# A two-layer NSA and MoBA trunk in fp32: values of two head pairs in one run, gate rows summed from parts, five raw buffers

## The chip, the cores and the metric

The kernel runs on one core of a Trainium2 chip. The metric is the device time of one execution in microseconds; the figure of before is the median of three runs. The profile shows five engines: TensorE (PE, with its weight loads as PEld), VectorE (DVE), ScalarE (ACT), GpSimd (POOL) and SyncE (SP), which issues most of the transfers.

## The reference

There are 256 tokens of width 1024 and two layers. Each layer takes shift, scale and gate from a condition vector (adaLN), normalizes x, runs a mixer and adds the gated result. Layer 0 is NSA attention (16 heads in 4 groups, with compressed keys and values, selected blocks and a window of 256); layer 1 is MoBA attention with one block of 256, so that its attention is causal attention over all 256 tokens.

```python
cond = jax.nn.silu(c)
for i in range(DEPTH):
    shift, scale, gate = jnp.split(cond @ ada_w[i] + ada_b[i], 3, axis=-1)
    h = rms_norm(x, norm_g[i]) * (1 + scale[:, None, :]) + shift[:, None, :]
    ...
        y = nsa_mixer(h, ...)   # layer 0
        y = moba_mixer(h, ...)  # layer 1
    x = x + gate[:, None, :] * y
# in a mixer
q, kc, vc, ks, vs, kw, vw, gl, z = split_cols(h @ w_in, [Q_W] + [KV_W] * 6 + [3 * N_HEADS, Q_W])
...
return gc[..., 0:1] * o_cmp + gc[..., 1:2] * o_slc + gc[..., 2:3] * o_win
...
return (o * jax.nn.silu(z)) @ w_out
```

## The kernel before

**Numbers.** Everything is fp32. A large product is made from two parts of each operand: a high part, rounded to the type fp32r (`hi`, a cast on ACT), and the rest (`lo`, a subtraction on DVE). Three products, high by high, high by low and low by high, are added up in PSUM. The weights come from HBM in pieces of 512 KB, 128 partitions by 1024 numbers, into the buffers `raw` (six of them) or, in the first quarter, `early`. `HT` holds the two parts of the transposed, normalized x; `qg` holds the parts of the gated attention output.

**Order.** No engine's program is written out by hand. The functions record operations, and `plan.issue` (L285 to L403) sets the order of each engine: it goes through simulated time, takes for each engine the operation that can start first, then by level (FIRST_OF_ALL, URGENT, CHAIN, FILL) and by key. The key is the number of the operation, shifted by the table `LATER_BY` (L42); the table `HOLD` (L55) gives some operations an earliest time. The operations of a `plan.group` stay together. Every recorded operation is emitted at one line, L406, so the profile tells them apart by tiles and not by lines. Buffers belong to rings (`plan.tag`, L480 on): 2 `acc` and 6 `ps` in PSUM, 6 `raw`, 4 `hi`, 4 `lo`, 5 `pT`. Which instruction stands where on an engine therefore depends on the tables, the ring sizes and the numbers of the operations.

**The start.** The lead loop (`for k in range(2)`, L1124) makes the scale and shift of the first 128 columns of layer 0, transposes the normalized x, writes its high part (ACT) and low part (DVE) to `HT`, and multiplies with the first pieces of `w_in`, which `parts_2d` (L1114) splits into two halves of 512 columns, each with a cast on ACT.

**Scale and shift.** `ada_ss` multiplies pieces of `ada_w` with `condz`, a column of the condition, in small products: the PE array is then used in tiles of 128 by 32 (the names `early,condz` and `raw,condz` in the profile).

**The gate row.** `ada_gate(l)` (L757) multiplies eight pieces of `ada_w` by the condition with eight scalar_tensor_tensor operations on DVE, which add up in the tile `gate` of 128 by 1024. Two fp32 products with a matrix of ones (`ps<-gate,ones`, 512 columns each) then sum it over the partitions, and ACT copies both halves back to `gate`. There is one gate row for each layer.

**Attention of layer 0.** There are 8 pairs of heads. `pair_a(i)` makes the scores (`KTA,qg`), the maxima and exponentials (DVE and ACT) and the transposed probabilities `pT`, and in the end calls `values` (`pT,VA`): eight fp32 products in array tiles of 128 by 64, which add to a PSUM tile that `Vbd` (`pcT,Vbd`, the compressed values) began; the tiles of two pairs are begun together. `gated` then multiplies with the z branch. The compression itself uses small products in tiles of 128 by 64 (`p,p` and `zT,p`).

**Layer 1** has the same frame without compression and selection: `pair_b` and `values_b`, then the products with `w_out`. After the last product the result is multiplied with the gate, added to x and written out.

Of the kernel before, what the change touches and what calls it, by code (L numbers as in the profile page):

```python
# [17 lines left out]
P = 128  # L18
# [38 lines left out]
    120: 16500, 167: 22100, 305: 52600, 312: 37600, 383: 32300, 385: 34800, 390: 48600, 395: 51100, 499: 79600,  # L57
    503: 79600, 951: 114700, 1239: 173400, 1371: 179400, 1543: 193600, 1558: 197000, 1625: 208400, 1715: 225000,
    1717: 227500, 1746: 205600, 2238: 273000,
# [13 lines left out]
class Plan:  # L73
# [159 lines left out]
    def _safe(tag, k):  # L233

        if k not in tag.known:
            held = tag.early | {k}
            end = max(tag.last[h] for h in held)
            tag.known[k] = all(
# [195 lines left out]
def kernel(  # L434
# [323 lines left out]
    def ada_gate(l):  # L758
# [10 lines left out]
        for s in range(2):  # L769
            t = tile_of("ps", 512)  # L770
            with plan.at(FILL):
                T.matmul(t, ones, gate[:, s * 512:(s + 1) * 512], start=True, stop=True)
                A.copy(gate[:, s * 512:(s + 1) * 512], t)
# [794 lines left out]
```

## Time and profile before

| | before |
|---|---|
| median of 3 runs | 308.71 us (308.33 to 309.14) |
| the profiled execution | 307.97 us |
| its span, from the first to the last instruction | 306.3 us |
| mean granted TensorE clock | 0.998 |
| PE busy | 297.5 us, 2097 records |
| PE weight loads busy | 242.2 us |
| DVE busy | 248.7 us, 736 instructions |
| ACT busy | 203.0 us, 484 instructions |
| transferred | 65.80 MB, mean 215 GB/s |

The profiled execution took 1.67 us more than its span: that lies ahead of the first and behind the last instruction. PE records overlap, since a product is drawn with its full latency: what a product costs in a stream is the distance from its start to the next start, not the length of its record. An fp32 product appears as two records in the timeline and as one row in the order of instructions.

### The profile page before, as it was taken

Reading aid. Unit: us, or ns where it says so; the run is one execution under the profiler, and the core shown is the slowest. Engines: PE = TensorE matmul, PEld = TensorE weight load, DVE = VectorE, ACT = ScalarE, POOL = GpSimd, SP = SyncE. Lnnn points to the kernel's source line nnn. Section 1 sums busy time; section 2 is a strip of 40 time slices with the busy share of each in tenths; the row PEclk is TensorE's granted clock in tenths of the full one; section 3 lists DMA queues with packets and bytes.
Section 4 is the critical chain, followed back from the end, with each engine's and each line's share of the span. In section 5 each row is a group of like instructions: output and inputs, shape, how many; then the busy total and the mean of one; then the engine's idle time right before and its main releaser. Section 6 shows DMA issues by size and latency. Waiting matters only on the chain.

```text
span 306.3 us, 6115 instructions
## 1 busy us (share of the span) xinstructions
PE 297.5 (97%) x2097; PEld 242.2 (79%) x2097; DVE 248.7 (81%) x736; ACT 203.0 (66%) x484; POOL 29.4 (10%) x100
## 2 busy tenths in 40 slices
PE   4999999999999999999999999999999999999995
PEld 4666777868878696878897788787788999878784
DVE  3674474678799988799999897797599999999664
ACT  4735244674937795679877985766566589999510
POOL 8128980000000000000000000000000000000000
PEclk9999999999999999999999999999999999999999
DMA  8999999699974294968558269036477780441002
GB/s 250 321 355 368 367 355 342 229 271 323 347 284 149 63 372 140 346 207 328 162 185 274 70 205 329 17 76 224 131 258 235 235 285 4 149 131 67 2 34 103
DMA packets 41099, 65.80 MB, mean 215 GB/s; under 512 B 4220, under 2 KB 20970, under 8 KB 41068
## 3 DMA queue, kind: packets, MB, share of 16 engines
q1 hardware_dynamic: 40708, 65.36, 65.0%
q8 instruction: 16, 0.26, 0.3%
q14 instruction: 15, 0.12, 0.1%
q10 hardware_dynamic: 168, 0.06, 0.1%
q0 software_dynamic: 192, 0.00, 0.0%
HBM read 64.36 MB, written 1.05 MB: 214 GB/s over the span
## 4 chain that ended last, share of the span: by engine, by line
PE 82%; DVE 6%; ACT 5%; DMA 4%; issue 2%; ACTq 0%; SPq 0%; DVEq 0%
PE ps L406 46%; PE acc L406 36%; DVE p L406 3%; ACT p L406 2%; DMA y<-in_ada_b_dram 2%; DMA early<-in_nsa_w_in_dram 1%; DMA raw<-in_nsa_w_out_dram 1%; DVE lo L406 1%; ACT pT L406 1%; ACT n_out L406 1%; DVE tiny L406 0%; ACT hi L406 0%; ACT HT L406 0%; ACT qg L406 0%; ACTq L406 0%
## 5 line engine op out<-in xcount | busy, mean ns | idle before, releaser
L406 ACT CAST hi<-raw 128x1024 fp32r<-128x1024 f32 (+1 forms) x48 | 49.2, 1027 | 17.1 <-PE acc L406 14.8
L406 DVE TENSOR_TENSOR lo<-raw,hi 128x1024 fp32r<-128x1024 f32 (+1 forms) x48 | 56.7, 1188 | 3.1 <-ACT hi L406 2.8
L406 ACT ACTIVATE p<-p,tiny 128x128 f32<-128x128 f32 (+1 forms) x96 | 43.2, 459 | 10.7 <-DVE tiny L406 10.6
L406 PE MATMUL acc<-hi,HT 128*128 128x512 f32 (+1 forms) x160 | 49.6, 383 | 0.0
L406 PE MATMUL acc<-HT,hi 128*128 128x256 f32 x192 | 39.1, 288 | 0.0
L406 PEld LDWEIGHTS acc<-hi,HT 128*128 128x128 f32 x160 | 28.8, 188 | 6.7 <-issue 1.2
L406 DVE CUSTOM_DVE_ANT_0 p<-ps,causal 128x128 f32<-128x128 f32 (+1 forms) x96 | 31.3, 356 | 1.5 <-PE ps L406 1.5
L406 PEld LDWEIGHTS acc<-HT,hi 128*128 128x128 f32 x192 | 30.5, 189 | 0.9 <-issue 0.7
L406 PE MATMUL acc<-lo,HT 128*128 128x512 f32 (+1 forms) x80 | 30.4, 384 | 0.4 <-DVE lo L406 0.4
L406 PE MATMUL ps<-hi,HT 128*128 128x512 f32 (+1 forms) x96 | 29.0, 367 | 0.0
L406 PE MATMUL ps<-KTA,qg 128*128 128x256 f32 (+2 forms) x192 | 27.3, 282 | 0.0
L406 PE MATMUL acc<-HT,lo 128*128 128x256 f32 x96 | 27.3, 286 | 0.0
L406 PEld LDWEIGHTS ps<-KTA,qg 128*128 128x128 f32 x192 | 24.2, 189 | 3.3 <-issue 1.2
L406 PE MATMUL ps<-hi,qg 128*128 128x256 f32 (+1 forms) x96 | 24.4, 324 | 0.0
L406 PE MATMUL acc<-hi,qg 128*128 128x512 f32 x64 | 23.3, 415 | 0.0
L406 ACT COPY pT<-ps 128x384 f32<-128x384 f32 x48 | 21.1, 492 | 2.3 <-PE ps L406 2.3
L406 DVE TENSOR_TENSOR lo<-early,hi 128x1024 fp32r<-128x1024 f32 (+2 forms) x17 | 17.4, 1041 | 5.4 <-ACT hi L406 5.0
L406 ACT CAST hi<-early 128x1024 fp32r<-128x1024 f32 (+2 forms) x17 | 14.8, 897 | 10.3 <-DMA early<-in_nsa_w_in_dram 8.5
L406 PE MATMUL ps<-identF,p 128*128 128x128 f32 x144 | 21.0, 275 | 0.2
L406 PEld LDWEIGHTS ps<-hi,HT 128*128 128x128 f32 x96 | 17.2, 188 | 4.6 <-issue 1.9
L406 DVE SCALAR_TENSOR_TENSOR gate<-raw,condz,gate 128x1024 f32<-128x1024 f32 x16 | 20.5, 1283 | 0.0
L406 PEld LDWEIGHTS ps<-identF,p 128*128 128x128 f32 x144 | 16.2, 140 | 3.8 <-DVE p L406 0.9
(218 smaller groups left out, 618.8 us busy)
## 6 DMA issues: line engine op xcount, KB each, us to landing
raw<-in_ada_w_dram SPq DMA_DIRECT2D x32, 512.0 KB, 5.7
raw<-in_moba_w_in_dram SPq DMA_DIRECT2D x20, 512.0 KB, 4.7
early<-in_ada_w_dram SPq DMA_DIRECT2D x12, 512.0 KB, 9.6
raw<-in_nsa_w_in_dram SPq DMA_DIRECT2D x12, 512.0 KB, 6.6
early<-in_nsa_w_in_dram SPq DMA_DIRECT2D x9, 512.0 KB, 9.2
raw<-in_nsa_w_out_dram SPq DMA_DIRECT2D x8, 512.0 KB, 4.6
raw<-in_moba_w_out_dram SPq DMA_DIRECT2D x8, 512.0 KB, 4.0
early<-in_nsa_w_in_dram SPq DMA_DIRECT2D x9, 256.0 KB, 6.0
```

The source lines that it names most:

```text
L406: r = getattr(self.engines[e], method)(*[self._real(a) for a in args], **{k: self._real(a) for k, a in kw.items()})
```

## The change

1. **Values of two pairs.** In layer 0 `pair_a` now ends with the transposed probabilities. `values_a` makes the values of two pairs: both `Vbd` products in one group, then all 16 value products in one group, then both `gated`. The ring `pT` grows from 5 to 8 buffers.
2. **Gate rows from parts.** `ada_gate` splits the gate tile into a high and a low part (one cast on ACT and one subtraction on DVE, 128 by 1024) and sums each half by two fp32r products with `onesR`, an fp32r copy of the ones, in place of one fp32 product.
3. **Five raw buffers** in place of six.
4. **High parts ahead of the second cast.** `parts_2d` takes `behind`: the cast of the second half of the first weight piece waits for the high part of `HT`.
5. Small tiles of the compressed keys (`kcm`, `TCc`, `TSc`, `kcy`) come from the ring `g`.
6. **The tables** `LATER_BY` and `HOLD` are replaced as a whole, and `_safe` takes several buffers at once.

The diff, cut to its core (of the two tables a line each):

```diff
 LATER_BY = [
-    (109, 110, -64), (255, 255, 155), (307, 310, -51), (316, 317, -56), (330, 330, 298), (350, 350, 26),
+    (41, 41, 123), (55, 55, -884), (135, 154, -101), (248, 248, -83), (249, 249, -67), (250, 250, -70),
...
 HOLD = {
-    120: 16500, 167: 22100, 305: 52600, 312: 37600, 383: 32300, 385: 34800, 390: 48600, 395: 51100, 499: 79600,
+    64: 8200, 120: 15900, 239: 26000, 388: 43700, 389: 47700, 390: 49400, 403: 44300, 473: 59600, 1110: 135300,
...
-    def _safe(tag, k):
+    def _safe(tag, *ks):
...
-                            blocked = len(free) < len(several)
+                            blocked = len(free) < len(several) or not self._safe(
+                                self.tags[name], *sorted(self.tiles[n]["place"] for n in several))
...
-    plan.tag("raw", work, 1024, 6)
+    plan.tag("raw", work, 1024, 5)
...
-            "pT": (384, 5, F32), "pcT": (256, 2, F32), "pc": (256, 2, F32), "g": (256, 2, F32)}
+            "pT": (384, 8, F32), "pcT": (256, 2, F32), "pc": (256, 2, F32), "g": (256, 2, F32)}
...
+    onesR = const.tile([P, P], F32R, name="onesR")
...
+        hi, lo = parts_of(gate.rearrange("p (s n) -> p s n", s=2))
         for s in range(2):
             t = tile_of("ps", 512)
             with plan.at(FILL):
-                T.matmul(t, ones, gate[:, s * 512:(s + 1) * 512], start=True, stop=True)
+                with plan.group():
+                    T.matmul(t, onesR, hi[:, s], start=True, stop=False)
+                    T.matmul(t, onesR, lo[:, s], start=False, stop=True)
                 A.copy(gate[:, s * 512:(s + 1) * 512], t)
...
-    def parts_2d(t, cuts, after=()):
+    def parts_2d(t, cuts, after=(), behind=()):
...
-                A.copy(hi[:, c0:c1], t[:, c0:c1])
+                with plan.at(URGENT if behind and c0 else FILL), plan.group(after=behind if c0 else ()):
+                    A.copy(hi[:, c0:c1], t[:, c0:c1])
...
+        if k:
+            with plan.at(FILL), plan.group(after=[plan.ops[-1]["id"]]):
+                V.tensor_copy(onesR, ones)
...
                 affine(HT[:, 0, k, toks], src, 0, k, A)
+                highs = [plan.ops[-1]["id"]]
...
-    kcm = const.tile([64, 96], F32, name="kcm")
+    small = tile_of("g", 240)[0:64]
+    kcm, TCc, TSc, kcy = small[:, 0:96], small[:, 96:160], small[:, 160:176], small[:, None, 176:240]
...
-        if j_ % 2 == 0:
-            with plan.group():
-                for j in range(j_, j_ + 2):
-                    ov[hf, j] = tile_of("ps", 512)
-                    T.matmul(ov[hf, j][:, 0:S], Vbd[32 * j:32 * j + 32, hf], pcT[hf][32 * j:32 * j + 32],
-                             start=True, stop=False, tile_position=(32 * j, 0))
-        o = ov[hf, j_]
-        vs = slice(g * HD, (g + 1) * HD)
-        values(o, [([VA[:, m, 1 - r, vs] for m in range(2)], pT[r]) for r in (1, 0)], False)
-        gated(i, o, zT[i])
+        return i, pT
+
+    def values_a(pairs):
+
+        os = {i: tile_of("ps", 512) for i, _ in pairs}
+        with plan.group():
+            for i in os:
+                hf, j = i // 4, i % 4
+                T.matmul(os[i][:, 0:S], Vbd[32 * j:32 * j + 32, hf], pcT[hf][32 * j:32 * j + 32],
+                         start=True, stop=False, tile_position=(32 * j, 0))
+        with plan.group():
+            for i, pT in pairs:
+                vs = slice(i // 2 * HD, (i // 2 + 1) * HD)
+                values(os[i], [([VA[:, m, 1 - r, vs] for m in range(2)], pT[r]) for r in (1, 0)], False)
+        for i in os:
+            gated(i, os[i], zT[i])
...
-        pair_a(i)
+        pairs = (pairs if i % 2 else []) + [pair_a(i)]
+        if i % 2:
+            values_a(pairs)
```

**Where instructions move.** Three places, read from the order in which each engine's program holds its instructions. The number behind a name tells the buffer of a ring: rows with the same number use the same buffer.

On PE, at the second and third pair of layer 0, the kernel before has eight value products, 14 other rows, and eight value products again. This is the first of these two runs with its neighbours (`raw,condz` are scale products of layer 1):

```order
L406 MATMUL acc_288<-HT,hi_341 128x256 x2
L406 MATMUL ps_245<-pT_1534,VA 64x256
L406 MATMUL ps_245<-pT_1409,VA 64x256
L406 MATMUL ps_245<-pT_1534,VA 64x128
L406 MATMUL ps_245<-pT_1409,VA 64x128
L406 MATMUL ps_245<-pT_1402,VA 64x256
L406 MATMUL ps_245<-pT_1414,VA 64x256
L406 MATMUL ps_245<-pT_1402,VA 64x128
L406 MATMUL ps_245<-pT_1414,VA 64x128
L406 MATMUL ps_158<-raw_643,condz 32x512 x2
```

The changed kernel has at the first two pairs, on PE, one run of sixteen, into two PSUM tiles; these are its last six rows on the first tile, the first four on the second, and what stands around them:

```order
L413 MATMUL ps_155<-pT_1310,VA 64x128
L413 MATMUL ps_155<-pT_1315,VA 64x128
L413 MATMUL ps_155<-pT_1321,VA 64x256
L413 MATMUL ps_155<-pT_1328,VA 64x256
L413 MATMUL ps_155<-pT_1321,VA 64x128
L413 MATMUL ps_155<-pT_1328,VA 64x128
L413 MATMUL ps_188<-pT_1393,VA 64x256
L413 MATMUL ps_188<-pT_1439,VA 64x256
L413 MATMUL ps_188<-pT_1393,VA 64x128
L413 MATMUL ps_188<-pT_1439,VA 64x128
```

The second pair's products now follow the first pair's at once, where before other work in another use of the array stood between them.

On ACT, at the start, the kernel before casts both halves of the first weight piece (`x2`) and then writes the high part of `HT` for the two token blocks:

```order
L406 ACTIVATE n_in_160<-X,rs_167 128x512
L406 ACTIVATE n_in_171<-X,rs_185 128x512
L406 CAST hi_241<-early_150 128x512 x2
L406 ACTIVATE HT<-ps_207,AB_114 128x128
L406 ACTIVATE HT<-ps_152,AB_114 128x128
L406 COPY n_out_272<-ps_207 128x3x128
```

In the changed kernel the same place on ACT reads:

```order
L413 ACTIVATE n_in_168<-X,rs_182 128x512
L413 CAST hi_243<-early_147 128x512
L413 ACTIVATE HT<-ps_204,AB_115 128x128
L413 ACTIVATE HT<-ps_188,AB_115 128x128
L413 CAST hi_243<-early_147 128x512
L413 COPY n_out_280<-ps_204 128x3x128
```

The second cast moved behind both high parts.

On ACT, at the end of the program, the kernel before has these last rows (the gate row was copied back earlier, and the casts are the last pieces of `w_out`):

```order
L406 COPY pT_1409<-ps_191 128x384
L406 COPY pT_1414<-ps_207 128x384
L406 CAST qg_1295<-g_1021 128x256
L406 CAST qg_1295<-g_999 128x256
L406 CAST hi_341<-raw_643 128x1024
L406 CAST hi_330<-raw_609 128x1024
```

In the changed kernel ACT ends so:

```order
L413 COPY gate_345<-ps_204 128x512
L413 CAST qg_1415<-g_991 128x256
L413 CAST qg_1415<-g_722 128x256
L413 COPY gate_345<-ps_204 128x512
L413 CAST hi_324<-raw_622 128x1024
L413 CAST hi_396<-raw_608 128x1024
L413 CAST hi_243<-raw_641 128x1024
```

The gate row's copies moved to the end, and three casts now stand behind the second of them; `hi_324` is the buffer that held the high part of the gate. On PE these are, in the changed kernel, the rows directly behind the last gate sum (which reads `hi_324` and `lo_264`), up to the first product with the new content of `hi_324`:

```order
L413 MATMUL acc_271<-hi_396,qg_1105 128x512
L413 MATMUL acc_271<-hi_243,qg_1118 128x512
L413 MATMUL acc_271<-lo_404,qg_1118 128x512
L413 MATMUL acc_271<-hi_243,qg_1118 128x512 x2
L413 MATMUL acc_271<-lo_404,qg_1118 128x512
L413 MATMUL acc_271<-hi_243,qg_1118 128x512
L413 MATMUL ps_188<-hi_304,qg_1105 128x256
L413 MATMUL ps_188<-lo_317,qg_1105 128x256
L413 MATMUL ps_188<-hi_304,qg_1105 128x256 x2
L413 MATMUL ps_188<-lo_317,qg_1105 128x256
L413 MATMUL ps_188<-hi_304,qg_1105 128x256
L413 MATMUL acc_267<-hi_324,qg_1415 128x512
```

So 13 products, seven of 512 columns and six of 256, stand between the last gate sum and the first product that needs the first of the three casts.

More of the change, by code (lines that the diff above doesn't have):

```diff
@@ L56 @@
 HOLD = {
-    120: 16500, 167: 22100, 305: 52600, 312: 37600, 383: 32300, 385: 34800, 390: 48600, 395: 51100, 499: 79600,
-    503: 79600, 951: 114700, 1239: 173400, 1371: 179400, 1543: 193600, 1558: 197000, 1625: 208400, 1715: 225000,
-    1717: 227500, 1746: 205600, 2238: 273000,
[3 rows of a table added]
 }
@@ L232, in _safe @@
     @staticmethod
-    def _safe(tag, k):
-        if k not in tag.known:
-            held = tag.early | {k}
+    def _safe(tag, *ks):
+        if ks not in tag.known:
+            held = tag.early.union(ks)
             end = max(tag.last[h] for h in held)
-            tag.known[k] = all(
-                sum(a not in held and a not in tag.done for a in tag.alive[b]) + len(held) <= tag.bufs
+            tag.known[ks] = all(
+                sum(a not in tag.done for a in tag.alive[b]) + sum(h > b for h in held) <= tag.bufs
                 for b in range(tag.next, len(tag.tiles)) if b not in held and b not in tag.given and tag.first[b] <= end)
-        return tag.known[k]
+        return tag.known[ks]
     @staticmethod
@@ L1141 @@
         a, b = lead_w[k]
-        w = [(p, sl) for p, cuts in ((parts_2d(a, (0, 512) if not k else (0,), known), (0, 512, 1024)), (parts_2d(b, (0,)), (0, 512, 768)))
+        w = [(p, sl) for p, cuts in ((parts_2d(a, (0, 512) if not k else (0,), known, highs), (0, 512, 1024)), (parts_2d(b, (0,)), (0, 512, 768)))
              for sl in (slice(c0, c1) for c0, c1 in zip(cuts, cuts[1:]))]
@@ L1271 @@
                      start=(m == 0), stop=(m == 1))
-    kcm = const.tile([64, 96], F32, name="kcm")
+    small = tile_of("g", 240)[0:64]
+    kcm, TCc, TSc, kcy = small[:, 0:96], small[:, 96:160], small[:, 160:176], small[:, None, 176:240]
     V.tensor_copy(kcm, cmp_ps[0:64, 0:96])
-    TCc = const.tile([64, HD], F32, name="TCc")
-    TSc = const.tile([64, 16], F32, name="TSc")
     V.tensor_copy(TCc[:, 16:64], NBc[:, 16:64])
@@ L1279 @@
     V.tensor_mul(TSc[:, 8:16], NBc[:, 0:8], kcm[:, 88:96])
-    kcy = const.tile([64, 1, HD], F32, name="kcy")
     norm_rope(kcm[:, None, 0:64], 1, 1, TCc[:, None, :], TSc[:, None, :], kcy)
@@ L1344, in pair_a @@
     def pair_a(i):
-        g, hf, j_ = i // 2, i // 4, i % 4
+        g = i // 2
         ps = []
```

28 rows, old and new, of tables (HOLD, LATER_BY) are left out of this document.

## The prediction

> **What bounds the kernel now.** I read the page first: the share of each engine, the slices and the chain.
>
> ```profile
> PE 297.5 (97%) x2097; PEld 242.2 (79%) x2097; DVE 248.7 (81%) x736; ACT 203.0 (66%) x484; POOL 29.4 (10%) x100
> PE   4999999999999999999999999999999999999995
> PEclk9999999999999999999999999999999999999999
> PE 82%; DVE 6%; ACT 5%; DMA 4%; issue 2%; ACTq 0%; SPq 0%; DVEq 0%
> ```
>
> PE is busy from the second slice to the next to last, its clock is full throughout, and the chain that ended last runs through PE for 82% of the span. Busy records overlap, so I then looked at what PE waits for. This is the whole view of its waits (total, times, longest):
>
> ```profile
> PE ps L406 <- DMA rot<-in_c_dram: 2.5, 1, 2.5
> PE ps L406 <- DMA X<-in_x_dram: 1.5, 1, 1.5
> PE acc L406 <- DVE lo L406: 0.4, 2, 0.2
> PE ps L406 <- DMA early<-in_ada_w_dram: 0.2, 1, 0.2
> ```
>
> 4.0 us are the first transfers, which the change does not touch; 0.6 us are left. So the kernel's time is PE's work plus a fixed start and tail, and an edit counts by what it does to the distances between PE's starts. The other engines matter where they have no room. The windows give PE, PEld, DVE, ACT and POOL in turn, in us of each stretch:
>
> ```profile
> 135.00:165.00 30.00, 29.80 (x259) 26.26 (x257) 30.00 (x100) 24.93 (x78) 0.00 (x0) 1.00 0.68 230
> 245.00:260.00 15.00, 15.00 (x140) 14.92 (x140) 15.00 (x62) 13.65 (x35) 0.00 (x0) 1.00 0.45 147
> 260.00:275.00 15.00, 14.89 (x108) 12.25 (x107) 15.00 (x50) 14.82 (x47) 0.00 (x0) 1.00 0.45 141
> 275.00:290.00 15.00, 15.00 (x113) 11.86 (x112) 13.19 (x50) 10.48 (x31) 0.00 (x0) 1.00 0.13 37
> 290.00:303.00 13.00, 12.63 (x72) 10.77 (x70) 7.84 (x12) 2.10 (x2) 0.00 (x0) 1.00 0.16 61
> ```
>
> DVE is full from 135 to 165 and from 245 to 275 us; there an operation more on DVE may show.
>
> **Gate rows from parts.** The timeline of PE shows, at 266.33, an fp32 sum (two records) and what follows it, and at 292.86 products of two fp32r operands, 512 columns each:
>
> ```profile
> 266.33 1.02 PE L406 MATMUL ps<-gate,ones 128*128 128x512 f32 x2
> 267.19 0.49 PE L406 MATMUL ps<-identF,p 128*128 128x128 f32 x3
> 292.86 0.40 PE L406 MATMUL acc<-lo,qg 128*128 128x512 f32 x1
> 293.09 0.63 PE L406 MATMUL acc<-hi,qg 128*128 128x512 f32 x2
> ```
>
> An fp32 sum takes 267.19 - 266.33 = 0.86 us of PE, an fp32r product 0.23 (293.09 - 292.86). Four sums at 0.86 are 3.44; eight products at 0.23 are 1.84: **-1.60 us**. ACT gets two casts and DVE two subtractions, by the groups of the same shape and the copies of the gate:
>
> ```profile
> L406 ACT CAST hi<-raw 128x1024 fp32r<-128x1024 f32 (+1 forms) x48 | 49.2, 1027 | 17.1 <-PE acc L406 14.8
> L406 DVE TENSOR_TENSOR lo<-raw,hi 128x1024 fp32r<-128x1024 f32 (+1 forms) x48 | 56.7, 1188 | 3.1 <-ACT hi L406 2.8
> L406 ACT COPY gate<-ps x4: 572/611/642, 169.0 to 269.0; 128x512 f32<-128x512 f32 x4
> ```
>
> That is 2 x 1.03 on ACT and 2 x 1.19 on DVE, beside PE's work while these engines keep ahead of it. I cost them at nothing, except at the end, below; uncovered, DVE's share is up to 2.4 us.
>
> A rule of the Trainium skill prices the new products otherwise: "TensorE: Matmul & The Clock Gate", Back-to-back issue gap, gives some 131 ns as the sustained spacing of products of 512 columns in a stream of loads and products. By it the eight would take 1.05 us and the saving would be 2.39. The rows above show 0.23 in just such a stream, so the measurement decides.
>
> **Values of two pairs.** A value run of before, with the flat product ahead of it and the one behind (each of the eight products has two records):
>
> ```profile
> 156.28 0.28 PE L406 MATMUL acc<-HT,lo 128*128 128x256 f32 x1
> 156.48 1.52 PE L406 MATMUL ps<-pT,VA 128*64 128x256 f32 x16
> 157.94 0.50 PE L406 MATMUL acc<-HT,hi 128*128 128x256 f32 x2
> ```
>
> The run takes 1.46, and the product ahead takes 0.20 where one of 256 columns takes half of 0.23, so entering costs 0.09. No run of sixteen value products is in this trace. What a run costs beyond its products I take from the two other kinds that occur short and long: the compression (`p,p` and `zT,p`, one run of 8 and one of 16) and the scale products (`early,condz`, 16 and 8):
>
> ```profile
> 72.32 1.08 PE L406 MATMUL ps<-p,p 128*64 128x256 f32 x8
> 73.23 1.03 PE L406 MATMUL ps<-zT,p 128*64 128x256 f32 x8
> 74.19 0.41 PE L406 MATMUL acc<-lo,HT 128*128 128x304 f32 x1
> ```
>
> ```profile
> 81.15 1.08 PE L406 MATMUL ps<-p,p 128*64 128x256 f32 x8
> ...
> 84.75 0.50 PE L406 MATMUL acc<-hi,HT 128*128 128x512 f32 x1
> ```
>
> ```profile
> 24.07 2.01 PE L406 MATMUL ps<-early,condz 128*32 128x256 f32 x32
> 26.00 0.49 PE L406 MATMUL ps<-hi,HT 128*128 128x512 f32 x1
> ```
>
> ```profile
> 47.37 1.07 PE L406 MATMUL ps<-early,condz 128*32 128x256 f32 x16
> 48.37 0.74 PE L406 MATMUL ps<-hi,HT 128*128 128x512 f32 x2
> ```
>
> Compression: 1.87 for 8 and 3.60 for 16, so two short runs cost 2 x 1.87 - 3.60 = 0.14 more, and 0.09 for the second entry: 0.23. Scale products: 2 x 1.00 - 1.93 = 0.07, and 0.09: 0.16. I take 0.23, since the compression's tiles have the value products' shape (128 by 64). By the order of instructions the twelve value runs of eight become five of sixteen and two of eight: five runs fewer, **-1.15 us** (-0.80 at 0.16).
>
> **What the new order does elsewhere.** The same order splits other runs: scale products stand in 16 runs for 12, the compression in 4 for 3, the `Vbd` products in 4 for 3. Six runs more, **+1.38** (+0.96 at 0.16). So merging and splitting together give +0.16 to +0.23, and the change's first part does not do what its words say: the number of times that PE changes its use of the array does not fall. PE's work alone falls by 1.60 - 0.23 = 1.37 us.
>
> **The start.** From the timelines of ACT and PE:
>
> ```profile
> 10.93 1.51 PE L406 MATMUL ps<-identF,n_in 128*128 128x128 f32 x12
> 11.35 0.62 ACT L406 CAST hi<-early 128x512 fp32r<-128x512 f32 x1 [0.52 <-DMA early<-in_nsa_w_in_dram]
> 11.88 0.80 ACT L406 ACTIVATE HT<-ps,AB 128x128 fp32r<-128x128 f32 x2
> 12.38 0.50 PE L406 MATMUL acc<-hi,HT 128*128 128x512 f32 x1
> ```
>
> With the second cast behind them, the high parts can start near 11.5. But the twelve transposes from 10.93 on keep PE until shortly before 12.38, so the first product gains about 0.1; the low parts, which wait for the high ones, gain up to 0.4 (11.88 against 11.5), and the view of waits has two waits of PE for `lo`, 0.2 the longest. Bounds 0 to -0.5; I take **-0.2 us**.
>
> **The end.** Behind the last gate sum the order holds seven products of 512 columns and six of 256, 7 x 0.23 + 6 x 0.115 = 2.30 us, and then the first that needs `hi_324`. On ACT a copy of the gate (0.61) and that cast (1.03) come first: 1.64, slack 0.66 without handovers. The second cast is due 0.46 later and takes 1.03: slack 0.09. The three subtractions on DVE, 1.19 each, follow with 0.2 to 0.4. A handover takes some 0.1 (the first `HT` part ends near 11.88 + 0.40, and the product that reads it starts at 12.38), and several lie on this chain: 0 to +0.7, I take **+0.3 us**.
>
> **Five raw buffers.** A transfer that waits for a buffer starts later by what the sixth gave. The closest place of before, on SP and ACT, and the largest group of SP's waits:
>
> ```profile
> 104.43 0.89 SPq L406 DMA_DIRECT2D raw<-in_nsa_w_in_dram  x2
> 108.41 1.05 ACT L406 CAST hi<-raw 128x1024 fp32r<-128x1024 f32 x1
> ...
> SPq L406 <- DVE lo L406: 73.3, 25, 13.4
> ```
>
> The first piece is cast 4.0 us after its issue, so it has no slack to speak of, and SP stood 25 times, 73.3 us in all, until a subtraction had freed a buffer: the buffers already hold the transfers back, and with five they do so earlier. From 0 to +1.0 (a piece late by one cast); I take 0, since PE waits for no raw piece in the view above. The `behind` group, the ring `g` and eight `pT` buffers add no PE work: 0.
>
> **The sum:** -1.60 - 1.15 + 1.38 - 0.20 + 0.30 = -1.27 us. The profiled execution took 307.97 (span 306.3, 1.67 around it), so it would take 306.70; the median of before is 308.71, 0.74 above it, so I predict **307.4 us**.
>
> **The rivals.** A measurement of this kernel can tell 0.3%, 0.93 us: faster is under 307.78, slower over 309.64.
>
> 1. *The forecast*, 307.4, chance 0.52; 0.08 of it falls above 307.78, where the start gives nothing and the end costs all its 0.7.
> 2. *The saved PE time turns into waits.* DVE has 2.4 us more and no room in two stretches, and raw pieces come later. If half of DVE's 2.4 us shows, the time is 307.4 + 1.2 = 308.6. For it: DVE 30.0 of 30.0 us. Against: PE waited for DVE only 0.4 us there and elsewhere. Chance 0.20, 0.03 of it beyond 309.64.
> 3. *Slower: the last gate row comes too late.* The order puts the last two multiply-adds of layer 1's gate, the cast and the subtraction into the last attention work, where DVE and ACT were full (245 to 275). PE's program holds both sums ahead of 61 products (31 x 0.23 + 30 x 0.115 = 10.6 us), which all wait with them. DVE's surplus there is 1.19 + 2 x 1.28 = 3.75 us (a multiply-add took 1.28, row below); shown in full the time is 307.4 + 3.75 = 311.2. It decides once 2.2 of these show. Against: from 275 to 303 DVE had 1.8 + 5.2 us free. Chance 0.10.
>
> ```profile
> L406 DVE SCALAR_TENSOR_TENSOR gate<-raw,condz,gate x16: 1252/1282/1302, 133.0 to 264.6; 128x1024 f32<-128x1024 f32 x16
> ```
>
> 4. *More gain:* the new order also removes PE's remaining small waits and the end costs nothing: 307.4 - 0.3 - 0.9 = 306.2. Chance 0.10; the view of waits leaves only 0.6 of such time.
> 5. *PE's work is not the bound*: what is removed was hidden, 308.7. Against it stand starts 0.23 apart without idle time. Chance 0.05. The Trainium skill ("Perfetto Trace Analysis", Identifying the Most-Contended Engine) says that the busy share of products is no measure and that the busy share of weight loads is; by it PE stands at 79%, below DVE.
> 6. *The fp32r products of one sum run closer than 0.23*, at half of it: 8 x 0.115 = 0.92 more saved, 306.5. No row shows it. Chance 0.03.
>
> Faster: 0.44 + 0.10 + 0.03 = 0.57. Within: 0.08 + 0.17 + 0.05 = 0.30. Slower: 0.03 + 0.10 = 0.13. The range reaches from 306.0 (below rival 4) to 309.4 (the forecast with the raw term of 1.0 and DVE's uncovered half); rival 3, 0.10, and ends of 2 and 4, together 0.08, are left out.
>
> **What would show it.** In the changed profile eight records of `hi,onesR` and `lo,onesR` 0.23 apart; a run of sixteen value products of about 2.8 us; PE's first product near 12.3; PE's waits still near 4.6 us in total, with new rows only at the end for `hi`, `lo` or `gate`. The forecast is wrong if PE waits for `raw`, `lo` or `gate` for over 1 us in the middle or the end, or if a run of sixteen takes as long as two of eight.

## The result, and the profile after

| | before | changed |
|---|---|---|
| median | 308.68 us (308.33 to 309.14, 4 runs) | 311.58 us (311.24 to 313.36, 4 runs) |
| the profiled execution | 307.97 us, span 306.3 | 311.24 us, span 309.5 |
| mean granted TensorE clock | 0.998 | 1.0 |

The changed kernel takes 1.0098 times the time of before, 95% interval 1.0071 to 1.0126: it is slower by 2.9 us. The prediction was 307.4, its range 306.0 to 309.4. These are the lines of the page of the changed kernel that answer to those of before: shares, slices and chain.

```profile
PE 299.2 (97%) x2097; PEld 243.2 (79%) x2097; DVE 252.0 (81%) x739; ACT 205.9 (67%) x486; POOL 28.2 (9%) x100
PE   4999999989999999999999999999999999999995
DVE  3665493659799999389999998896699999999665
PE 75%; DVE 12%; DMA 6%; ACT 2%; issue 2%; SPq 2%; ACTq 0%; DVEq 0%
```

PE's share has not moved, but the chain that ended last now runs through DVE for 12% of the span (6% before). The whole view of PE's waits (total, times, longest) in the changed kernel:

```profile
PE ps L413 <- POOL selC L555: 2.5, 1, 2.5
PE ps L413 <- DMA X<-in_x_dram: 1.4, 1, 1.4
PE ps L413 <- DVE p L413: 0.9, 1, 0.9
PE acc L413 <- ACT HT L413: 0.5, 1, 0.5
PE ps L413 <- ACT pT L413: 0.3, 1, 0.3
PE acc L413 <- DVE zT L413: 0.3, 1, 0.3
PE ps L413 <- DVE tiny L413: 0.3, 1, 0.3
PE acc L413 <- DVE lo L413: 0.2, 1, 0.2
```

They sum to 6.4 us against 4.6 before. That is 1.8 more, while the profiled execution is 3.27 longer and PE's work was to shrink. So this view does not hold the whole loss: it counts only gaps between records, and records overlap.

**A measure that sees the waits.** I gave each row of PE's order the distance that its kind takes in a stream (0.23 for 512 columns, half of it for 256, the value and scale runs as in the prediction) and added these up along the program. That sum is PE's work; the time at which a row starts, minus the work ahead of it, is its lag. Work is 284.26 us before and 282.95 in the changed kernel: **-1.31**, where the prediction had -1.37. The lag at the last product is 18.21 before and 22.78 after: **+4.57**. The difference, 3.26, is the 3.27 of the profiled executions. Lag in us, by the work done:

| PE work done | before | changed |
|---|---|---|
| 45 | 9.73 | 10.11 |
| 55 | 9.84 | 11.70 |
| 125 | 12.23 | 14.12 |
| 135 | 13.06 | 14.69 |
| 155 | 14.11 | 17.62 |
| 175 | 14.70 | 18.05 |
| 185 | 15.16 | 19.13 |
| 245 | 16.64 | 21.46 |
| 275 | 18.04 | 22.59 |
| 282 | 18.15 | 22.77 |

Against before, the changed kernel loses 1.5 between 45 and 55, 1.9 between 135 and 155, 0.6 between 175 and 185, 0.9 spread over 185 to 245, and nothing to speak of at the end; between these stretches it regains some tenths. The first two of these losses are looked at below; for the third and fourth (1.5 together) no run was made, and their cause is open. Up to 45 us of work even profiles of kernels with the same order differ: PE's 301st record starts between 45.55 and 46.95 us in the eight kernels (before and seven of the experiments below) that share the order of before. So lags are compared from there on. From that record to the 801st, these eight take 70.93 to 71.09 us, so behind the start some 0.2 us can be told.

**The first loss** lies at 61 to 65 us of the trace, where ACT and DVE copy 16 blocks of the compression out of PSUM. Of the changed kernel, the DVE timeline and the PE timeline:

```profile
63.21 0.40 DVE L413 COPY p<-ps 64x224 f32<-64x224 f32 x1 [1.71 <-ACT p L413]
64.09 1.08 DVE L413 COPY p<-ps 64x256 f32<-64x256 f32 x3 [0.48 <-ACT p L413]
```

```profile
64.57 0.66 PE L413 MATMUL ps<-identF,zT 128*128 128x128 f32 x4 [0.87 <-DVE p L413]
```

and the same place on DVE before:

```profile
61.29 1.39 DVE L406 COPY p<-ps 64x224 f32<-64x224 f32 x4 [1.40 <-PE ps L406]
```

Before, DVE makes four copies in one piece. In the new order ACT and DVE take turns: DVE waits for ACT in the rows above, and at 64.57 PE waits for DVE.

**The second loss** lies where the softmax of layer 0 is. Two stretches with nearly the same PE work, in both of which DVE is never idle, are 138.7 to 169.3 in before (30.6 us) and 139.2 to 172.7 in the changed kernel (33.5 us). By the lags above the first holds 28.7 to 29.6 us of PE work and the second 30.0, so that 0.4 to 1.3 of the 2.9 us between them is work and the rest lag. The windows of before (PE, PEld, DVE, ACT, POOL in turn, then the granted clock and the transfers):

```profile
150.00:155.00 5.00, 5.00 (x45) 4.92 (x44) 5.00 (x20) 4.54 (x11) 0.00 (x0) 1.00 0.66 204
155.00:160.00 5.00, 5.00 (x47) 4.39 (x46) 5.00 (x18) 2.85 (x11) 0.00 (x0) 1.00 0.59 199
sum 30.60, PE 30.40 PEld 26.01 DVE 30.60 ACT 25.59 POOL 0.00; mean PE 5.07 PEld 4.34 DVE 5.10 ACT 4.26 POOL 0.00
```

and of the changed kernel:

```profile
150.00:155.00 5.00, 4.74 (x36) 3.79 (x37) 5.00 (x28) 5.00 (x20) 0.00 (x0) 1.00 0.78 257
155.00:160.00 5.00, 4.68 (x36) 3.89 (x36) 5.00 (x18) 5.00 (x19) 0.00 (x0) 1.00 0.35 119
sum 33.50, PE 32.62 PEld 27.38 DVE 33.50 ACT 29.31 POOL 0.00; mean PE 4.66 PEld 3.91 DVE 4.79 ACT 4.19 POOL 0.00
```

DVE does 2.9 us more and ACT 3.7 more in the second stretch, and from 150 to 160 both are full there. What the more is, the groups of these two stretches tell. Before, on DVE and ACT:

```profile
L406 DVE SCALAR_TENSOR_TENSOR gate<-raw,condz,gate 128x1024 f32<-128x1024 f32 x5 | 6.4, 1286 | 0.0
```

```profile
L406 ACT COPY pT<-ps 128x384 f32<-128x384 f32 x12 | 5.5, 474 | 0.6 <-PE ps L406 0.5
```

In the changed kernel:

```profile
L413 DVE SCALAR_TENSOR_TENSOR gate<-raw,condz,gate 128x1024 f32<-128x1024 f32 x8 | 10.2, 1273 | 0.0
L413 DVE TENSOR_TENSOR lo<-gate,hi 128x1024 fp32r<-128x1024 f32 x1 | 1.2, 1218 | 0.0
```

```profile
L413 ACT COPY pT<-ps 128x384 f32<-128x384 f32 x18 | 8.1, 484 | 0.9 <-PE ps L413 0.7
L413 ACT CAST hi<-gate 128x1024 fp32r<-128x1024 f32 x1 | 1.1, 1052 | 0.4 <-DVE gate L413 0.4
```

Eight multiply-adds of the gate instead of five and its subtraction stand in the stretch, 5.0 us more on DVE (other work there is less, which leaves 2.9), and 18 copies of probabilities instead of 12 on ACT. The order packs more of their work beside nearly the same PE work.

### The profile page after: what moved, and what is told of

The parts are those of the page before. It is cut to its first block, busy times and chain, and to the rows that moved or that the text cites. A ratio compares the mean times of both kernels' runs of the same rounds, so it can differ in the third digit from the quotient of the medians.

```text
span 309.5 us, 6121 instructions
## 1 busy us (share of the span) xinstructions
PE 299.2 (97%) x2097; PEld 243.2 (79%) x2097; DVE 252.0 (81%) x739; ACT 205.9 (67%) x486; POOL 28.2 (9%) x100
## 3 DMA queue, kind: packets, MB, share of 16 engines
HBM read 64.36 MB, written 1.05 MB: 211 GB/s over the span
## 4 chain that ended last, share of the span: by engine, by line
PE 75%; DVE 12%; DMA 6%; ACT 2%; issue 2%; SPq 2%; ACTq 0%; DVEq 0%
PE ps L413 41%; PE acc L413 34%; DVE p L413 5%; DMA early<-in_nsa_w_in_dram 3%; DVE gate L413 2%; DMA early<-in_ada_w_dram 2%; DMA y<-in_ada_b_dram 2%; SPq L413 2%; DVE lo L413 1%; DVE tiny L413 1%; DVE zT L413 1%; ACT hi L413 1%; DVE qg L413 0%; ACT p L413 0%; DVE g L413 0%
## 5 line engine op out<-in xcount | busy, mean ns | idle before, releaser
L413 ACT CAST hi<-raw 128x1024 fp32r<-128x1024 f32 (+1 forms) x48 | 48.5, 1022 | 17.8 <-PE acc L413 15.0
L413 PE MATMUL acc<-hi,HT 128*128 128x512 f32 (+1 forms) x160 | 50.6, 384 | 0.0
L413 DVE CUSTOM_DVE_ANT_0 p<-ps,causal 128x256 f32<-128x256 f32 (+1 forms) x96 | 29.7, 348 | 2.8 <-PE ps L413 2.6
L413 PE MATMUL acc<-hi,qg 128*128 128x512 f32 x64 | 22.0, 400 | 0.3 <-DVE zT L413 0.3
L413 ACT ACTIVATION_READ_ACCUMULATOR p<-p,tiny 128x1 f32 x96 | 19.1, 199 | 0.0
```

Of the source, the lines that this page charges most:

```text
L413: r = getattr(self.engines[e], method)(*[self._real(a) for a in args], **{k: self._real(a) for k, a in kw.items()})
```

## The experiments

The kernels were made so: each engine keeps its rows in the order of before (names with `b_`) or of the changed kernel (`a_`), from a list that replaces the planner's choice, and only what is named differs. Lag growth is the lag at 282 us of work minus that at 45: 8.42 before, 12.66 in the changed kernel. The medians were taken in several sessions, in which before stood at 308.22 to 308.97, so kernels are compared by their ratios to the before of their own session; the changed kernel has 1.0098 (1.0071 to 1.0126).

**b_gatePE: the shorter sums alone, in before's order.**

```diff
-                T.matmul(t, ones, gate[:, s * 512:(s + 1) * 512], start=True, stop=True)
+                with plan.group():
+                    T.matmul(t, halfR, g[:, s * 512:(s + 1) * 512], start=True, stop=False)
+                    T.matmul(t, halfR, g[:, s * 512:(s + 1) * 512], start=False, stop=True)
```

> The kernel before, every engine's instructions in the order of before, with one edit: the last multiply-add of each gate row writes the row as fp32r, and each half is summed by two fp32r products with a matrix of one half in place of one fp32 product with ones. The low part of the gate is left out; no cast and no subtraction is added. If the term of the sum is right (four sums of 0.86 us become eight products of 0.23 us on the engine that bounds the kernel): 308.7 - 1.6 = 307.1 us. If PE's work there does not set the time: 308.7 us.

Measured 308.66 (307.93 to 310.26, 10 runs), ratio 0.9996, interval 0.9979 to 1.0013. PE's work falls by 1.60 (284.26 to 282.66), and the lag grows by 10.01 for 8.42: all of it is waited out. The weight loads of layer 0's sums show how; in this kernel the two halves of the first gate row are (PEld timeline)

```profile
167.39 0.30 PEld L537 LDWEIGHTS ps<-n_parts,halfR 128*128 128x128 f32 x2
...
168.64 0.30 PEld L537 LDWEIGHTS ps<-n_parts,halfR 128*128 128x128 f32 x2 [0.71 <-DVE tiny L537]
```

1.25 apart, the second held 0.71 by DVE, whose work frees its PSUM buffer. In before, the two fp32 sums stand just as far apart (PE timeline), and the second one's load had a wait too (PEld timeline):

```profile
166.40 1.13 PE L406 MATMUL ps<-gate,ones 128*128 128x512 f32 x2
...
167.65 1.12 PE L406 MATMUL ps<-gate,ones 128*128 128x512 f32 x2
...
167.65 0.30 PEld L406 LDWEIGHTS ps<-gate,ones 128*128 128x128 f32 x2 [0.52 <-DVE tiny L406]
```

The long records had covered a wait for a buffer, and a shorter sum uncovers it.

**b_gateDVE: the cast and the subtraction alone, unused.**

```diff
+        hi, lo = tile_of("n_parts", D), tile_of("n_parts", D)
+        with plan.at(FILL):
+            A.copy(hi, gate)
+            V.tensor_sub(lo, gate, hi.bitcast(F32))
```

> The kernel before, in the order of before, with only the added work of the gate's parts: one cast on ACT and one subtraction on DVE behind the last multiply-add of each gate row, whose results nothing uses; the sums stay fp32. Theory LOAD (the added 2 x 1.19 us on DVE and 2 x 1.03 us on ACT find no room where DVE is full): 308.7 + 1.2 to 2.4 = 309.9 to 311.1 us. Theory ORDER (the changed kernel loses its time to the places at which the new order puts instructions, not to this work): within 0.5 of 308.7 us.

Measured 311.12 (310.17 to 311.58), ratio 1.0067 (1.0047 to 1.0086): about +2.1 to +2.3, near DVE's 2 x 1.19. ACT's two casts are in this run as well, and it does not part them from DVE's subtractions. The load that the prediction cost at nothing shows nearly in full in this order.

**b_gate and b_gate2: the whole second edit in before's order.** The diff is that of change 2; in b_gate2 the subtraction stands some 1.3 us behind the cast and not directly behind it.

> The kernel before (308.8) with the whole second edit: gate rows summed from a high and a low part by eight products in place of four fp32 sums, with the cast, the subtraction and the copies, the sums 12 TensorE rows later than before's so that the parts are there; order and all else as before. From the two runs of its halves (0.0 for the shorter sums, +2.3 for the cast and the subtraction) LOAD expects 310.3 to 311.3: the edit by itself costs about as much as the whole change. If the shorter sums pay once the parts are there, 309.0 to 310.0. The prediction's sum would have it at 307.1.

> b_gate with other places for the gate's parts: the subtraction not directly behind its cast but some 1.3 us later, the sums 12 TensorE rows behind it, the copies six rows behind the sums. Theory LOAD: the cast and the subtraction still cost the 2.3 they cost unused, the shorter sums give 0 to 1.6: 309.5 to 311.1. Theory PLACE (b_gate's 5.5 were waits for its parts): the same range or lower, down to the prediction's 307.1 if the load is hidden as well. If it stays above 312.5, parts as such are too late in this order, wherever they are put nearby.

Measured 313.90 (313.29 to 314.71), ratio 1.0178 (1.0154 to 1.0203), and 315.39 (313.82 to 315.80), ratio 1.0197 (1.0162 to 1.0232). b_gate misses every range given; b_gate2 misses the ranges of its theories, and its third case came, that parts are too late in this order wherever they are put nearby. The edit costs more than twice what its halves did. In b_gate PE's work is 1.60 less, and the lag jumps by 3.7 at layer 0's sums (145 to 155 us of work) and by 4.0 at layer 1's (245 to 255), where before has 0.6 and 0.4. Three rows of its PE timeline:

```profile
164.86 0.73 PE L537 MATMUL ps<-KTA,qg 128*128 128x256 f32 x4 [1.22 <-ACT pT L537]
...
270.46 0.50 PE L537 MATMUL ps<-n_parts,onesR 128*128 128x512 f32 x1 [0.67 <-ACT n_parts L537]
271.71 0.49 PE L537 MATMUL ps<-n_parts,onesR 128*128 128x512 f32 x1 [0.76 <-DVE n_parts L537]
```

At 164.86 PE waits for a copy of probabilities that the gate's cast (163.4, 1.05 us) holds up on ACT; at 270.46 for the cast itself; at 271.71 for the subtraction. These waits are the load and the place together; the two runs do not part them further. The 1.5 us between b_gate2 and b_gate are no measure of the place: in the profile of b_gate2 the granted TensorE clock (the third number from the end) stands at half from 272.0 to 278.8, with waits of PE for DVE of 0.39, 0.94 and 1.39 us around its start (269 to 273.3), and all four of its runs have a mean clock of 0.987 to 0.992.

```profile
272.00:279.00 7.00, 5.70 (x20) 5.01 (x21) 6.38 (x24) 4.02 (x11) 0.00 (x0) 0.51 0.26 83
```

**a_fp32gate: the changed kernel with the fp32 sums back, without cast and subtraction.**

```diff
-        hi, lo = parts_of(gate.rearrange("p (s n) -> p s n", s=2))
-                with plan.group():
-                    T.matmul(t, onesR, hi[:, s], start=True, stop=False)
-                    T.matmul(t, onesR, lo[:, s], start=False, stop=True)
+                T.matmul(t, ones, gate[:, s * 512:(s + 1) * 512], start=True, stop=True)
```

> The changed kernel, in its own order, with the gate rows summed by fp32 products as before, without the cast and the subtraction. ORDER: its waits stay, and the saved 1.6 us of PE come back: 311.6 + 1.6 = 313.2 us. LOAD: the waits between 134 and 172 us go with the subtraction, 311.6 + 1.6 - 2.4 = 310.8 us or less.

Measured 312.84 (312.41 to 314.22), ratio 1.0137 (1.0109 to 1.0166): some 1.2 above the changed kernel, though the two intervals overlap. In the profiles PE's work rises by 1.59 and the lag growth stays (12.59 for 12.66). In this order, which holds the sums back until the parts are there, the shorter sums are worth about what the prediction said, and taking the cast and the subtraction away gains nothing. The same arithmetic is thus worth about -1.2 in one order and +5.5 in the other.

**a_copies and a_start60: the early losses.** a_copies gives ACT its copies at 58 to 66 us in the order of before; of ACT's rows:

```diff
 COPY zT<-acc 128x512
-COPY p<-ps 64x32x8
 COPY zT<-acc 128x512
...
 COPY VA<-ps 128x256
+COPY p<-ps 64x32x8
 COPY p<-ps 64x32x7
```

a_start60 gives all operations of the first 60 us before's order.

> The changed kernel, in its own order but for one place: the copies on ACT and DVE that take the transposed blocks for the compression out of PSUM, near 58 to 66 us, stand as in the kernel before (all of one buffer on DVE, then all of it on ACT, instead of one by one in turn). ORDER: the wait of PE for a copy near 64 us (0.9 us) and its fore-runners go, 311.6 - 1.3 = 310.3 us. If the time there is lost to something else, a late transfer or a late weight: 311.6 us, with another releaser at the same place.

> The changed kernel with the operations of its first 60 us in the order of before, the rest as it is. Theory ORDER (each of the changed order's losses stands by itself, and stays in the total): the loss of the start, 0.4 us by the lag at 45 us of work, and a part of the 1.4 us at the copies around 62 us go: 310.0 to 311.2. Theory SLACK (a later stretch sets the time, and what is won ahead of it is waited out): 311.3 to 311.8.

a_copies: 311.59 (310.22 to 313.15), ratio 1.0092 (1.0059 to 1.0126). Its profile shows the wait of 0.87 for DVE gone and 0.50 for an ACT copy in its place; from 45 to 55 us of work the lag grows 0.93 for 1.59, and the growth to the end is 11.98: the 0.7 stays won in the profiled execution, and the median, with runs 3 us apart, does not show it. So less than half of the first loss is shown to come from the order of ACT's copies. a_start60: 310.96 (310.52 to 311.73), ratio 1.0084 (1.0061 to 1.0107), with a lag growth of 12.61. The median lies in the range of ORDER, but its interval also holds the ratio of the changed kernel: the start of the new order is no proven loss.

**b_short, b_shortPE, a_short: DVE's gate work cut.** Seven of the eight multiply-adds of each gate row are cut to one column, which leaves most of the gate row out; DVE's work on the gate falls by 15 us (26.92 us of busy time before, 11.88 in b_short).

```diff
-                V.scalar_tensor_tensor(gate, w, condz[:, kk, 0:1], gate, op0=OP.mult, op1=OP.add)
+                n = D if kk == 7 else 1
+                V.scalar_tensor_tensor(gate[:, 0:n], w[:, 0:n], condz[:, kk, 0:1], gate[:, 0:n], op0=OP.mult, op1=OP.add)
```

> The kernel before, in its own order, with seven of the eight multiply-adds of each gate row cut to one of 1024 columns: this leaves out most of the gate rows' sum over the condition; every instruction, load and wait is still there, but DVE has 14 x 1.2 = 16.8 us less to do, half of it in 127 to 170 us and half before 265 us. Theory DVE (in these two stretches DVE, which never stands there, sets the time, and PE fills in around it): 308.8 - 1 to 2 = 307.3 us or less. Theory PE (PE sets the time throughout): within 0.4 of 308.8 us.

> As the one with the short multiply-adds on the kernel before, and with the eight fp32r products in place of the four fp32 sums (no cast, no subtraction). DVE: with DVE out of the way the 1.6 us of PE that were worth 0.2 alone are now worth 1.2 to 1.6 us against the kernel with short multiply-adds. If they are hidden for another reason: no difference to it.

> The changed kernel, in its own order, with the same seven of eight multiply-adds of each gate row cut to one column. DVE: the waits of PE between 145 and 172 us go, 311.6 - 2.5 to 3.5 = 308.1 to 309.1 us; what is left against the short version of before is the waits for copies near 61 us and at 200 us, less the saved PE time. ORDER (the places of the instructions cost time whatever DVE has to do): 311 us or more.

b_short 307.61 (306.63 to 310.09), ratio 0.9969 (0.9946 to 0.9993). b_shortPE, with the shorter sums of b_gatePE besides: 307.10 (306.63 to 309.72), ratio 0.9964 (0.9942 to 0.9985), only 0.5 less than b_short, where theory DVE expected 1.2 to 1.6. Its PEld timeline shows why:

```profile
167.08 0.30 PEld L537 LDWEIGHTS ps<-n_parts,halfR 128*128 128x128 f32 x2 [0.71 <-DVE tiny L537]
```

The second sum of layer 0 is held as long as in b_gatePE, by work of the softmax (`tiny`), and not by the gate's multiply-adds. At layer 1 the loads of the two sums stand 0.79 apart (265.38 and 266.17), for 1.17 in b_gatePE (267.19 and 268.36): that 0.4 is most of the 0.5.

a_short 310.72 (310.04 to 312.47), ratio 1.0074 (1.0050 to 1.0099): some 0.8 less than the changed kernel, with overlapping intervals, and far from the 308.1 to 309.1 of theory DVE. So 15 us less on DVE are worth 1.0 in before's order (interval 0.2 to 1.7) and about as much, within the noise, in the new one. What remains in a_short, its windows show (this profile is of the slowest of its five runs, with the granted clock at half from 107.6 to 111.0, so its lags are not used):

```profile
150.00:155.00 5.00, 5.00 (x40) 3.20 (x38) 5.00 (x25) 4.54 (x18) 0.00 (x0) 1.00 0.60 193
155.00:160.00 5.00, 5.00 (x41) 4.54 (x40) 5.00 (x27) 5.00 (x20) 0.00 (x0) 1.00 0.69 234
```

ACT is all but full there (9.54 of 10 us) without any change to it, and DVE still is full, with the softmax and one subtraction of a weight piece. PE is busy throughout. DVE's load from the gate is thus at most a part of the second loss.

**a_dve, a_dve2, a_dve5, a_both: an earlier entry into the full stretch.** In the changed kernel DVE idles for some 6 us between 124 and 136 us. a_dve moves work into it; of PE's rows:

```diff
 MATMUL ps<-raw,condz 32x512 x2
+MATMUL ps<-KTA,qg 128x256 x4
 MATMUL ps<-pT,VA 64x256
...
 MATMUL ps<-pcT,Vbd 128x256
-MATMUL ps<-KTA,qg 128x256 x4
 MATMUL acc<-HT,hi 128x256
```

> The changed kernel (311.6), all tables as they are, but three moves between 123 and 138 us: on TensorE four scores of the next pair stand ahead of the first value run of sixteen and the compressed scores right behind it (they stood behind two other runs); on VectorE the scalings of probabilities that are ready by then stand ahead of the gating with z; on ScalarE the exponential of the compressed scores stands ahead of one z activation. Theory DVE (VectorE idles some 6 us between 124 and 136 us, although it sets the time from about 139 to 172): idle of 1 to 2 us there is filled, the lag at the second gate sum falls by as much, 309.8 to 310.6. Theory PE (what TensorE does between 118 and 165 us sets the time, VectorE's idle is harmless): 311.3 to 311.9.

> As the run before, and the eight groups of transposes of these probabilities on TensorE, with their copies on ScalarE, also stand 5 to 8 us earlier, and the second pair of Vbd products stands right ahead of its value run. Theory DVE: as the run before or up to 0.5 less, 309.5 to 310.6; if the copies hold the PSUM buffers up, up to 0.5 more. Theory PE: 311.3 to 312.

> The changed kernel (311.6) with the moves of a_dve, and besides: four transposes of ready probabilities spread among the z products from 131 us on, their copies where ScalarE was idle (130.8 to 134.2), and the three groups of scores that stood at 138.6, 142.1 and 142.9 us up to 6 us earlier; the second pair of Vbd products right ahead of its value run. Theory SCORES (in a_dve the win was waited out at 143 us for the scores; TensorE's order starts the full stretch late): the lag between 135 and 165 us of TensorE work grows 0.7 to 1.5 less than after's 3.1, total 310.0 to 311.0. Theory CHAIN (inside the stretch VectorE, ScalarE and six PSUM buffers hold each other up, whenever it starts): growth 2.8 to 3.4, total 311.3 to 312.

> a_dve5, and the 16 copies of the compression around 62 us in the order of before, as in a_copies, whose lag fell by 0.7 there. If losses in series add up: 0.5 to 0.8 under a_dve5. If what is won early is waited out later: as a_dve5 within 0.3.

a_dve: 311.93 (310.83 to 313.92), ratio 1.0120 (1.0075 to 1.0165); a_dve2: 314.18 (312.78 to 314.89), 1.0183 (1.0144 to 1.0222), outside all its ranges; a_dve5: 311.40 (310.76 to 313.11), 1.0087 (1.0054 to 1.0121); a_both: 311.07 (310.36 to 311.93), 1.0066 (1.0039 to 1.0092). In a_dve DVE's idle time up to 139 us of the trace, added up, falls from 39.7 to 37.4, and the lag growth is 12.64: no gain. Its DVE timeline shows where the win went, and that of a_dve5, which brings the scores up to 6 us forward, shows the next hold:

```profile
143.06 0.42 DVE L538 CUSTOM_DVE_ANT_0 p<-ps,causal 128x256 f32<-128x256 f32 x1 [0.88 <-PE ps L538]
```

```profile
141.79 1.28 DVE L538 SCALAR_TENSOR_TENSOR gate<-raw,condz,gate 128x1024 f32<-128x1024 f32 x1 [0.82 <-DMA raw<-in_ada_w_dram]
```

First DVE waits for scores that PE's order holds at 142 us; with these early, for the gate's first piece from HBM. In before the first multiply-add ran at 133.0, in the changed kernel at 142.03. In a_dve5 the lag grows by 2.94 from 135 to 155 us of work, for 2.93: CHAIN, not SCORES. In a_dve2 the lag growth is 15.36; some 1.1 of the 2.7 more come between 66 and 95 us, ahead of its moves. That the early transposes fill PSUM buffers while ACT is busy is our guess for the rest, not shown. a_both adds the copies of a_copies: growth 11.65, and 0.66 of the 1.01 falls where a_copies had it. So what a_copies won is won again in the lags; by the medians a_both and a_dve5 overlap. No run of these came back to before.

**b_lopool and a_lopool: 14 subtractions of the full stretches on GpSimd.**

```diff
-            V.tensor_sub(lo, t, hi.bitcast(F32))
+            (G if plan.ops[-1]["id"] + 1 in BY_POOL else V).tensor_sub(lo, t, hi.bitcast(F32))
```

> The kernel before (308.8), its order unchanged, 14 of the subtractions that make low parts of weight pieces (5 between 149 and 163 us, 9 between 230 and 274 us, 1.2 us each on VectorE) on GpSimd instead, which is idle there. Theory DVE: 17 us less on VectorE in its full stretches, like b_short, whose cut of about 18 us gave 1.2: 307.2 to 308.2. What speaks against it: GpSimd's time for such a subtraction is not in any trace here; its widest subtraction-like row (128 by 144, 0.33 to 0.50 us) gives 2.3 to 3.5 us for 1024 columns. If low parts come late or GpSimd slows VectorE by as much: 309 to 312.

> The same on the changed kernel (311.6): 14 subtractions of its two full stretches on GpSimd. Theory DVE: like a_short, 310.0 to 311.0. Theory CHAIN (ScalarE and the PSUM buffers are as full): 311.2 to 311.9. If low parts come late: 312 or more.

b_lopool 319.08 (318.29 to 320.77), ratio 1.0347 (1.0321 to 1.0373); a_lopool 332.45 (331.64 to 336.52), ratio 1.0790 (1.0746 to 1.0833). Both are far worse than the theories had it, and b_lopool lies outside every range given; what DVE does beside GpSimd is in the section on the hardware. In a_lopool the granted clock adds to it: the profile has half the clock for 3.4, 3.4 and 10.2 us (from 152, 166 and 258 us on), and its six runs have 0.968 to 0.978. No version that does all the work came out ahead of before; b_shortPE, which leaves work out, gains 0.4% (0.6% at most by its interval) in before's order.

## Why the prediction was wrong

1. **PE's work: right.** -1.37 was forecast, -1.31 came. The sums from parts run 0.23 apart and a run of sixteen value products takes 127.06 - 124.31 = 2.75 (about 2.8 forecast), as the changed kernel's PE timeline shows:

```profile
124.31 2.82 PE L413 MATMUL ps<-pT,VA 128*64 128x256 f32 x32
127.06 1.07 PE L413 MATMUL ps<-raw,condz 128*32 128x512 f32 x8
...
294.45 0.40 PE L413 MATMUL ps<-hi,onesR 128*128 128x512 f32 x1
294.68 0.39 PE L413 MATMUL ps<-lo,onesR 128*128 128x512 f32 x1
294.91 0.62 PE L413 MATMUL acc<-hi,qg 128*128 128x512 f32 x2
```

Rival 6, closer spacing, falls with the last three rows.

2. **"So the kernel's time is PE's work plus a fixed start and tail": the step that failed.** It rested on 0.6 us of waits. b_gatePE took 1.60 us of PE's work away and next to nothing else, and the time stayed. The view of waits was blind to what long fp32 records covered; the idle time ahead of the weight loads (0.52 us at the second sum of before, above) was in the trace and was not looked at. The waits that the prediction named as a sign of being wrong (over 1 us for `raw`, `lo` or `gate`) belong to the same view and did not show: PE waits 0.2 for `lo` in the changed kernel, and never for `raw` or `gate`.

3. **"I cost them at nothing, except at the end": mis-sized in before's order.** It named the full stretches of DVE and then let PE's wait of 0.4 us outweigh them. b_gateDVE measured 2.1 to 2.3. In the new order this work costs nothing by itself (a_fp32gate); whether that order paid for the room elsewhere is not shown.

4. **"What the new order does elsewhere" was priced by runs alone.** It counted entries into array tiles (+1.38) and nothing else of an order that was replaced as a whole. The 4.57 us of lag are there: 1.5 at the copies, 1.9 in the softmax of layer 0, 1.5 behind it, 0.4 at the start, less some tenths between. This is the largest term, and it has no line in the sum. The runs found where it lies; they took back 0.7 of it (a_copies) and did not show the cause of the rest.

5. **The start and the end.** PE's first product came at 12.43, for 12.38 before, so the -0.2 did not come. From 275 to 282 us of work the lag grows 0.18, for 0.11 before: the +0.3 at the end did not come either, and rival 3, whose 311.2 lies near the time, had the wrong place.

6. **Rival 2** (the saved time turns into waits, 308.6) named the mechanism. Its price, half of DVE's 2.4, was far too low, and it held only the gate's own load, not the order's packing. Rival 5 (what is removed was hidden, 308.7, chance 0.05) is what b_gatePE measured for the shorter sums in before's order.

7. **Five raw buffers** cost at 0 is open. SP stood longer for subtractions, in the changed kernel

```profile
SPq L413 <- DVE lo L413: 94.6, 32, 9.0
```

for 73.3 us and 25 times before. The first multiply-add of the gate ran at 142.0 (133.0 before) and that of layer 1 at 215.7, for 210.9, here behind a wait for its piece (DVE timeline):

```profile
215.70 1.28 DVE L413 SCALAR_TENSOR_TENSOR gate<-raw,condz,gate 128x1024 f32<-128x1024 f32 x1 [1.90 <-DMA raw<-in_ada_w_dram]
```

PE never waited for a piece, and DVE never did in before. No run changed the number of buffers alone; before with five was not run.

What else stays open: why the new order packs the softmax of layer 0 more tightly. The run of sixteen needs all eight `pT` buffers at once and so gathers two pairs' copies; that is an argument from the order, and no run undid the pairing alone.

## What to carry to other kernels

When PE is busy for 97%, look at the idle time ahead of its weight loads and take one piece of PE's work away in a trial before pricing savings by PE's spacing: here 1.6 us less work was worth nothing in one order and about 1.2 in another. When a schedule is replaced as a whole, compare what each other engine does beside the same amount of PE work, by stage. Where two engines are full together, relief for one can leave the other: removing 15 us from DVE was worth about 1 here. Look at the granted clock of every run before explaining its time.

## What the runs showed of the hardware

GpSimd is no free place for VectorE's work here. In b_lopool, two subtractions run on POOL from 152.17 on, and four scalings on DVE beside them take 5.37 us (POOL timeline, then DVE timeline):

```profile
152.17 5.02 POOL L538 TENSOR_TENSOR lo<-raw,hi 128x1024 fp32r<-128x1024 f32 x2 [1.73 <-ACT hi L538]
```

```profile
152.23 5.37 DVE L538 TENSOR_SCALAR p<-p,tiny 128x256 f32<-128x256 f32 x4
...
159.58 1.13 DVE L538 TENSOR_SCALAR p<-p,tiny 128x256 f32<-128x256 f32 x4
```

The same four take 1.13 at 159.58, where POOL is idle: DVE stands until POOL is about done (157.19). A small product of two inputs, 128 by 16, which takes 0.17 at 251.05, took 2.41 beside a subtraction of POOL from 252.06 to 254.72:

```profile
252.34 2.41 DVE L538 TENSOR_TENSOR rs<-rs 128x16 f32<-128x16 f32 x1
```

Not every operation is held: from 148.06 to 150.44 POOL works too, and DVE's operations on PSUM (`p<-ps,causal`, 0.42 each) run at their usual pace. A subtraction takes POOL 2.49 us in the mean (14 of them) and DVE 1.22. With 17 us of subtractions moved away, DVE's busy time rose, from 248.7 to 253.1 us in the page of b_lopool:

```profile
PE 298.5 (94%) x2097; PEld 241.9 (76%) x2097; DVE 253.1 (80%) x722; ACT 203.6 (64%) x484; POOL 64.2 (20%) x114
```

The Trainium skill ("SBUF — State Buffer", Who interferes with whom) says that some VectorE operations share a port pair with GpSimd, that a scaling of this kind in its fast mode is one, and that the one that comes second is blocked for the whole instruction. The rows of the scalings agree.

The granted clock of TensorE fell to half within three of the profiles, for 6.8 us in b_gate2 (row above), 3.4 us in a_short and 17 us in all in a_lopool. In b_gate2 waits of PE lie around its start; in a_short PE was busy for all of the 7 us before. What sets it off, no run here shows.
